# The steps of the 32x32 inversion on GpSimd instead of VectorE, in a hybrid decoder block

## Chip, cores and metric

The kernel runs on one core of a Trainium2 chip. The metric is the device time of one execution in microseconds (us). An execution under the hardware profiler gives the trace; its own time stands beside its span below. The engines are TensorE (PE; its weight loads are PEld), VectorE (DVE), ScalarE (ACT), GpSimd (POOL), and SyncE (SP), whose queue here only issues DMAs.

## What is computed

One layer of a decoder on 256 tokens and 16 meta tokens in front of them (L = 272), width 2048, all in float32. After a normalisation one large projection feeds three branches: RWKV-7 time mixing (16 heads of 64), a forgetting attention (FoX, 16 heads of 64) and gates. The two branches are projected, gated, added, projected again, and a SwiGLU network of width 5632 follows.

```
xn = rms(h, n1);  proj = xn @ w_in
y_a = rwkv7(...);  y_b = fox(...)
h = h + (g_a * (y_a @ w_a) + g_b * (y_b @ w_b)) @ w_o
h = h + (silu(gate) * up) @ w_dn          # gate, up = rms(h, n2) @ w_gu
```

The core of rwkv7 is a scan over tokens; for each head with a 64x64 state S:

```
sa = einsum('bhvk,bhk->bhv', S, a_t)
S  = S*w_t + sa*b_t + v_t*k_t
y_t = einsum('bhvk,bhk->bhv', S, r_t)
```

## The kernel before

**Projections.** Weights come from HBM in jobs. `wload` (L299) issues the DMA of a block of 128x1024 into `raw` on SP's queue (L318), makes a rounded copy `wh` on ScalarE (L322) and the remainder `wl` on VectorE (L323). `raw`, `wh` and `wl` have three buffers each. TensorE then multiplies with both parts (L333 to L335, L391 to L394). `run` (L377) loads the next job before it multiplies the last one.

**The recurrence.** The scan is done in chunks of 64 tokens, and each chunk needs the inverse of a unit triangular 64x64 matrix. The heads are taken in four groups `g` of four heads; a group has 16 such matrices (4 heads x 4 chunks) and 4 smaller ones for the meta tokens. For each group `rwkv_jobs(g)` (L615) runs the projections, and then `rwkv_bg(g)` (L670) runs as a stream in the background of the later projections: `slot` (L361) gives a stream a turn between TensorE's jobs, and each `yield` names the nanoseconds after which the stream is due again. So the order of TensorE's instructions is written by hand (`tc.manual_schedule`, L289). Outside the first stage, the order on the other engines, with SP's queue and GpSimd's, is laid out when the program is built.

**The inversion of the diagonal blocks.** In `rwkv_bg`:

- L765 to L773: the masked matrices `NK` go through DRAM (`d1`) into `ln`, so that each of 112 partitions holds one 32x32 block (1024 values). Three partition groups of 32 hold the same 32 blocks, one for each third of the result's rows; the last 16 hold the meta blocks.
- L830: GpSimd copies unit rows from `lunit` to `lx`, the result, with 11 rows of 32 in each partition.
- L831 to L838: 31 steps of forward substitution. Step `s_` multiplies column `s_` of the first n = s_//3+1 rows with row `s_` of the block into `lt` (L834), and adds that to the n rows in `lx` (L836). Both work on n lines of w = 31-s_ elements in 112 partitions. Every instruction needs the one before it.
- L841 to L848: the result goes through DRAM (`d2`, `d3`) into the 64x64 inverse `X` and `X0` for the meta tokens: seven DMAs out, six back, all on SP's queue.
- L913: VectorE transposes part of `X` into `XT`. L920 (`QT`) and L928 complete the off-diagonal blocks on TensorE; `step` (L854) then runs the recurrence. The line of most of these matmuls in the profile is that of the helper `pe_mm` (L355).

**Other work of GpSimd around the steps.** The copies of `NK` (L776, L780), the bonus term (L791), the biases and masks of the attention (L1067 to L1070, twice in a group), zeroing of tiles (L716, L738, L797, L828, L829), and the differences `zd` for the token shift (L445), which VectorE's L448 uses. At the start of the kernel it makes masks (L129, L138, L152, L154).

**Other work of VectorE there.** wl (L323), the sums of gate halves `zg` (L399, one operand in PSUM), scores and their division (L1087, L1098), and the scaling of the next group's projections (L437).

Of the kernel before, what the change touches and what calls it, by code (L numbers as in the profile page):

```python
# [13 lines left out]
ALU = mybir.AluOpType  # L14
# [42 lines left out]
LANES = 112  # L57
# [40 lines left out]
def hybrid_block(ctx, tc, A, out, dbg=None):  # L98
    nc = tc.nc
# [515 lines left out]
    def rwkv_jobs(g):  # L615
# [24 lines left out]
        def mul(w):  # L640
            (uh, ul), (gh, gl) = w
            gg = box["gg"] = ot(f"gg{g}")
            for m in range(2):
                ms = slice(m * P, (m + 1) * P)
                ps = main_ps(f"g{g}{m}")[:, :T]
                for k in range(2):
                    mm3(ps, gh[:, k, ms], gl[:, k, ms], sgh[:, k, :], sgl[:, k, :], k == 0, k == 1)
                nc.vector.tensor_copy(gg[:, m, :], ps)
            for nm, i, dh, dl, bname in (("sig", 0, twh, twl, "w0"), ("aa", 1, adh, adl, "a0")):
                dst = box[nm] = et(f"{nm}{g}")  # L650
                for m in range(2):
                    ms = slice(m * P, (m + 1) * P)
                    ps = (aux_ps if i == 0 else main_ps)(f"{nm}{g}{m}")[:, :L]
                    mm3(ps, uh[:, i, ms], ul[:, i, ms], dh, dl, True, True)
                    nc.scalar.activation(dst[:, m, :], ps, AF.Sigmoid, bias=vc(bname, 2 * g + m))
            spawn(rwkv_bg(g, box), HOP)
# [13 lines left out]
    def rwkv_bg(g, box):  # L670
# [91 lines left out]
        ln = rw.tile([LANES, 32, 32], F32, tag="ln", name=f"ln{g}", bufs=1)  # L762
# [62 lines left out]
        lx = rw.tile([LANES, 11, 32], F32, tag="lx", name=f"lx{g}", bufs=1)  # L825
# [5 lines left out]
        for s_ in range(31):  # L831
            n, w = s_ // 3 + 1, 31 - s_
            tv, xv = lt[:, 0:n, s_ + 1:], lx[:, 0:n, s_ + 1:]
            nc.vector.tensor_tensor(tv, lx[:, 0:n, s_:s_ + 1].to_broadcast([LANES, n, w]),  # L834
                                ln[:, s_:s_ + 1, s_ + 1:].to_broadcast([LANES, n, w]), op=ALU.mult)
            nc.vector.tensor_tensor(xv, xv, tv, op=ALU.add)  # L836
            if s_ % 4 == 3:
                yield STEP  # L838
        for j in range(3):
            n = 11 if j < 2 else 10  # L840
# [550 lines left out]
```

## Time and profile before

| | us |
|---|---|
| median of 3 runs | 1566.58 (1565.39 to 1569.84) |
| the profiled execution | 1564.75 |
| its span | 1563.0 |
| GpSimd (POOL) busy | 104.3 |
| VectorE busy | 1015.7 |
| ScalarE busy | 766.8 |
| instructions L834 and L836 | 124 each, 168 to 781 ns and 181 to 681 ns, between 123.8 and 536.8 us |

The page of the profile gives the busy time of each engine as a share of the span. The chain of waits is followed back from the last instruction, at each step to what released it. Groups of instructions have a line, an engine, the operation, out<-in by the program's names with the shapes, a count, then the busy time in us and the mean of one in ns, then the idle time ahead of them. The rows of a timeline have start in us, duration in us (of all, where "xN" follows), engine, line and operation. A row of the table by stage has the stretch, its length, the busy time of TensorE with its instructions, the granted clock, the share of the DMA engines and GB/s. "SPq" is SP's queue; its durations are those of issuing.

### The profile page before, as it was taken

The page shows a single profiled execution, that of the slowest core. Times are in us where ns is not written, and L with a number is a line of the kernel's source. Part 1 is how long each engine was busy: PE and PEld are TensorE (multiplying, and loading weights), DVE is VectorE, ACT ScalarE, POOL GpSimd, SP SyncE. Part 2 cuts the span into 40 slices and gives each one's busy share as a digit, 9 for nine tenths or more (in the row PEclk, how much of TensorE's full clock was granted, in tenths as well). Part 3 has the DMA queues.
Part 4 walks back from the last instruction along what each step waited for, and adds up shares of the span by engine and source line. Part 5 has one row for each costly group of instructions (what it writes and reads, how often), then busy time and mean ns, then how long its engine had stood idle before and what let it go on. Part 6 is the DMA issues. An engine that isn't in the chain of part 4 may idle for free.

```text
span 1563.0 us, 26173 instructions
## 1 busy us (share of the span) xinstructions
PE 1553.5 (99%) x10225; PEld 1366.3 (87%) x10225; DVE 1015.7 (65%) x1854; ACT 766.8 (49%) x1118; POOL 104.3 (7%) x194
## 2 busy tenths in 40 slices
PE   9999999999999999999999999999999999999998
PEld 9999988989889888999888888888888888888887
DVE  7878688677768856875655666566566656444443
ACT  6655455465445544654445554454445544333332
POOL 2121103102203100000000000000000000000000
PEclk9999999999999999999999999999999999999999
DMA  7556546546545566777666666666666666666664
GB/s 243 173 154 173 158 126 179 157 119 168 166 135 148 161 182 192 248 225 227 189 182 179 188 186 190 188 188 189 188 189 189 185 193 187 188 202 199 187 200 131
DMA packets 211483, 283.33 MB, mean 181 GB/s; under 512 B 23888, under 2 KB 128352, under 8 KB 211360
## 3 DMA queue, kind: packets, MB, share of 16 engines
q1 hardware_dynamic: 206752, 277.53, 60.8%
q10 hardware_dynamic: 4608, 4.13, 0.8%
q8 instruction: 80, 1.31, 0.4%
q14 instruction: 43, 0.35, 0.1%
HBM read 274.43 MB, written 7.19 MB: 180 GB/s over the span
## 4 chain that ended last, share of the span: by engine, by line
PE 94%; DVE 3%; DMA 1%; ACT 1%; issue 1%; SPq 0%; POOL 0%; DVEq 0%; ACTq 0%
PE up L392 10%; PE gt L392 10%; PE zg L392 7%; PE dn L1255 5%; PE dn L1253 5%; PE dn L1254 5%; PE up L394 5%; PE gt L394 5%; PE zg L394 3%; PE f L333 2%; PE f L392 2%; PE f L335 2%; PE f L334 2%; PE br L334 2%; PE br L335 2%; PE br L333 2%
## 5 line engine op out<-in xcount | busy, mean ns | idle before, releaser
L323 DVE TENSOR_TENSOR wl<-raw,wh 128x1024 fp32r<-128x1024 f32 (+1 forms) x496 | 605.3, 1221 | 439.7 <-ACT wh L322 437.8
L322 ACT ACTIVATE wh<-raw 128x1024 fp32r<-128x1024 f32 (+1 forms) x496 | 521.2, 1052 | 624.5 <-PE dn L1254 144.4
L392 PE MATMUL gt<-hts,wh 128*128 128x512 f32 x704 | 245.0, 394 | 0.0
L392 PE MATMUL up<-hts,wh 128*128 128x512 f32 x704 | 244.9, 394 | 0.0
L394 PE MATMUL gt<-hts,wl 128*128 128x256 f32 x660 | 186.2, 282 | 0.0
L394 PE MATMUL up<-hts,wl 128*128 128x256 f32 x660 | 186.0, 282 | 0.0
L392 PE MATMUL zg<-xhl,wh 128*128 128x512 f32 x512 | 184.3, 403 | 0.0
L392 PEld LDWEIGHTS up<-hts,wh 128*128 128x128 f32 x704 | 130.1, 188 | 26.4
L392 PEld LDWEIGHTS gt<-hts,wh 128*128 128x128 f32 x704 | 130.1, 188 | 26.3
L1254 PE MATMUL dn<-wh,acl 128*128 128x512 f32 x352 | 139.5, 396 | 0.0
L1253 PE MATMUL dn<-wh,ach 128*128 128x512 f32 x352 | 139.5, 396 | 0.0
L1255 PE MATMUL dn<-wl,ach 128*128 128x512 f32 x352 | 139.5, 396 | 0.0
L394 PE MATMUL zg<-xhl,wl 128*128 128x256 f32 x480 | 135.0, 281 | 0.0
L394 PEld LDWEIGHTS up<-hts,wl 128*128 128x128 f32 x660 | 124.7, 189 | 1.8
L394 PEld LDWEIGHTS gt<-hts,wl 128*128 128x128 f32 x660 | 124.7, 189 | 1.8
L392 PEld LDWEIGHTS zg<-xhl,wh 128*128 128x128 f32 x512 | 94.5, 188 | 20.8 <-issue 1.8
L394 PEld LDWEIGHTS zg<-xhl,wl 128*128 128x128 f32 x480 | 90.6, 189 | 1.1
L1255 PEld LDWEIGHTS dn<-wl,ach 128*128 128x128 f32 x352 | 66.3, 188 | 16.2
L1254 PEld LDWEIGHTS dn<-wh,acl 128*128 128x128 f32 x352 | 66.3, 188 | 16.2
L1253 PEld LDWEIGHTS dn<-wh,ach 128*128 128x128 f32 x352 | 66.3, 188 | 16.1
L333 PE MATMUL f<-xhl,wh 128*128 128x272 f32 x256 | 77.7, 303 | 0.0
L335 PE MATMUL f<-xhl,wl 128*128 128x272 f32 x256 | 73.8, 288 | 0.0
(459 smaller groups left out, 2777.6 us busy)
## 6 DMA issues: line engine op xcount, KB each, us to landing
raw<-in_w_gate_up_dram SPq DMA_DIRECT2D x176, 512.0 KB, 3.6
raw<-in_w_in_dram SPq DMA_DIRECT2D x160, 512.0 KB, 4.2
raw<-in_w_down_dram SPq DMA_DIRECT2D x88, 512.0 KB, 4.7
raw<-in_w_o_dram SPq DMA_DIRECT2D x32, 512.0 KB, 4.6
raw<-in_w_branch_a_dram SPq DMA_DIRECT2D x16, 512.0 KB, 3.9
raw<-in_w_branch_b_dram SPq DMA_DIRECT2D x16, 512.0 KB, 3.8
zgd<-zg ACTq DMA_DIRECT2D x30, 128.0 KB, 2.4
gate<-zgd SPq DMA_DIRECT2D x15, 256.0 KB, 5.8
```

The costliest lines, as they stand in the source:

```text
L322: nc.scalar.activation(wh[:prow, cs_], raw[:prow, cs_], AF.Copy)
L323: nc.vector.tensor_tensor(wl[:prow, cs_], raw[:prow, cs_], wh[:prow, cs_].bitcast(F32), op=ALU.subtract)
L333: nc.tensor.matmul(ps, wh, ah, start=first, stop=False)
L334: nc.tensor.matmul(ps, wh, al, start=False, stop=False)
L335: nc.tensor.matmul(ps, wl, ah, start=False, stop=last)
L392: nc.tensor.matmul(ps.rearrange("p (a t) -> p a t", a=2), wh, act, start=first, stop=last)
L394: nc.tensor.matmul(ps[:, :T], wl, act[:, 0, :], start=False, stop=False)
L1253: nc.tensor.matmul(box[t], ah[:, kt, ts_], wh[:, k, :], start=first, stop=False)
L1254: nc.tensor.matmul(box[t], al[:, kt, ts_], wh[:, k, :], start=False, stop=False)
L1255: nc.tensor.matmul(box[t], ah[:, kt, ts_], wl[:, k, :], start=False, stop=last)
```

## The change

The two instructions of each of the 31 steps are issued on GpSimd. Their operands, shapes and order stay as they are, and so does all else in the source: the copy to `lx` ahead of them, the yields, and the DMAs behind them.

```diff
         for s_ in range(31):
             n, w = s_ // 3 + 1, 31 - s_
             tv, xv = lt[:, 0:n, s_ + 1:], lx[:, 0:n, s_ + 1:]
-            nc.vector.tensor_tensor(tv, lx[:, 0:n, s_:s_ + 1].to_broadcast([LANES, n, w]),
-                                ln[:, s_:s_ + 1, s_ + 1:].to_broadcast([LANES, n, w]), op=ALU.mult)
-            nc.vector.tensor_tensor(xv, xv, tv, op=ALU.add)
+            nc.gpsimd.tensor_tensor(tv, lx[:, 0:n, s_:s_ + 1].to_broadcast([LANES, n, w]),
+                                    ln[:, s_:s_ + 1, s_ + 1:].to_broadcast([LANES, n, w]), op=ALU.mult)
+            nc.gpsimd.tensor_tensor(xv, xv, tv, op=ALU.add)
             if s_ % 4 == 3:
                 yield STEP
```

## The prediction

> **What bounds the kernel now.** I read the page first, for who is busy.
>
> ```profile
> span 1563.0 us, 26173 instructions
> ...
> PE 1553.5 (99%) x10225; PEld 1366.3 (87%) x10225; DVE 1015.7 (65%) x1854; ACT 766.8 (49%) x1118; POOL 104.3 (7%) x194
> ```
>
> TensorE (PE) is busy for 1553.5 of 1563.0 us. All its idle time together is 9.5 us, start included, so that is the most that any change away from TensorE can win. VectorE (DVE) at 65% is not the bound. Second, the chain of waits around the inversion. In the third of the four head groups it leaves TensorE:
>
> ```profile
> 406.38 0.19 DVE lx L836
> ...
> 406.59 0.61 SPq L841
> ...
> 411.74 1.69 DMA X<-d
> ...
> 415.48 4.61 DMA raw<-in_w_in_dram
> ...
> 420.19 1.06 ACT wh L322
> 421.25 0.41 ACT pT L1110
> 421.66 0.04 issue
> 421.71 1.41 PE po L355 x10
> ```
>
> This is read from top to bottom: the last step of the inversion releases the DMAs of the inverse on SP's queue; a weight load (raw, L318) stands behind them there; ScalarE waits for that load with wh, pT stands behind wh, and TensorE waits for pT. So the inversion's end already touches the path, through SP. Third, the table by stage shows what that costs:
>
> ```profile
> 416.00:455.00 39.00, 37.34 (x401) 1.00 0.57 166
> ```
>
> TensorE is idle for 1.66 of 39 us in that group, at full clock (1.00). This is the largest hole that an earlier end of the inversion could close.
>
> **What is removed.** Each group runs 31 steps of a multiplication and an addition. The groups of VectorE's instructions in the first group's inversion, from 123 to 153.4 us:
>
> ```profile
> L323 DVE TENSOR_TENSOR wl<-raw,wh 128x1024 fp32r<-128x1024 f32 x10 | 12.2, 1220 | 4.3 <-ACT wh L322 4.3
> L836 DVE TENSOR_TENSOR lx<-lx,lt 112x84 f32<-112x84 f32 (+23 forms) x31 | 7.6, 247 | 0.6
> L834 DVE TENSOR_TENSOR lt<-lx,ln 112x84 f32<-112x84 f32 (+23 forms) x31 | 7.6, 245 | 0.6
> L399 DVE TENSOR_TENSOR zg<-zg,zg 128x256 f32<-128x256 f32 x4 | 1.7, 417 | 1.3 <-ACT zg L398 1.3
> ```
>
> VectorE loses 15.2 us of work per group, 61 us in four. I put that at nothing: the 9.5 us above bound what it could give, and of the place shown it could give 1.66 us, if the weight load there came earlier.
>
> **What is added: the price of a step on GpSimd (POOL).** The shape of step s is n lines of w elements with n = s//3+1 and w = 31-s. Over the 31 steps that makes 1991 elements and 176 lines, twice (L834 and L836): 62 instructions, 3982 elements, 352 lines. The nearest rows of GpSimd are its other two-input operations and one that works on short lines:
>
> ```profile
> L445 POOL TENSOR_TENSOR zd<-z x24: 612/640/1611, 52.3 to 445.7; 128x272 f32<-128x272 f32 x16, 128x256 f32<-128x256 f32 x8
> ```
>
> ```profile
> 399.08 0.74 POOL L1070 TENSOR_TENSOR bias<-bias,cmask 128x256 f32<-128x256 f32 x1
> ```
>
> ```profile
> L138 POOL TENSOR_SCALAR_AFFINE_SELECT mup<-mup 64x64 f32<-64x64 f32 x4 | 0.8, 236 | 0.1
> ...
> L154 POOL TENSOR_SCALAR_AFFINE_SELECT lunit<-lunit 16x256 f32<-16x256 f32 x1 | 0.7, 732 | 0.1
> ...
> L129 POOL TENSOR_SCALAR_AFFINE_SELECT cmask<-cmask 128x128 f32<-128x128 f32 x1 | 0.3, 293 | 0.0
> ```
>
> In L445 (duration: least, median, most) I read 612 ns as the 256-element form and 640 as the 272-element form: 1.75 ns an element and 164 ns beside. Without a price for lines, 62 x 0.164 + 3982 x 0.00175 = 17.1 us: the lower end. L1070 does 256 elements in two lines, with a broadcast operand as in L834, in 0.74 us: 0.128 us more for one more line. 352 - 62 = 290 further lines at that price are 37 us: 54 us, the upper end. Between them lies the affine select: 293 - 236 ns for 64 more elements is 0.89 ns each, so 256 in one line would take 0.407 us; L154 does them in eight lines of 32 in 0.732, which is 0.047 us for each further line. I take that, because lines of about 32 elements are what the steps have: 290 x 0.047 = 13.6, in all 31 us for a group left alone, twice VectorE's own time. A step that waits for the one before it has its gap in this by counting whole durations, although unrelated instructions of GpSimd start a little before the last one ends.
>
> **It is not left alone.** The same instruction as above, in the first group, and what VectorE did then:
>
> ```profile
> 145.73 1.88 POOL L1070 TENSOR_TENSOR bias<-bias,cmask 128x256 f32<-128x256 f32 x1
> ```
>
> ```profile
> 145.79 1.21 DVE L323 TENSOR_TENSOR wl<-raw,wh 128x1024 fp32r<-128x1024 f32 x1
> ```
>
> 1.88 against 0.74 us: 1.14 longer, nearly the whole of the wl that ran beside it. So GpSimd stands while wl runs. Which of VectorE's other work stops it? Beside wl (L323) and zg (L399) of the rows above, the division of the scores (L1098) is there:
>
> ```profile
> L1098 DVE TENSOR_SCALAR s<-s,sums 128x144 f32<-128x144 f32 (+1 forms) x4 | 1.3, 322 | 0.0
> ```
>
> ```profile
> 397.31 1.11 POOL L1067 TENSOR_SCALAR bias<-bias,cq,hs 128x272 f32<-128x272 f32 x2
> ```
>
> ```profile
> 397.88 0.41 DVE L399 TENSOR_TENSOR zg<-zg,zg 128x256 f32<-128x256 f32 x1
> ```
>
> L399, which reads one operand from PSUM, kept its 0.41 us inside a busy stretch of GpSimd, so I count only wl and L1098: 12.2 + 1.3 = 13.5 of 30.4 us, 44%. GpSimd keeps 56%, and 31 us become 55. Were L399 to stop it too, it would be 15.2 of 30.4, a pace of 0.50.
>
> The Trainium skill (SBUF — State Buffer, Who interferes with whom) says the same against this change: VectorE and GpSimd share one pair of ports under a lock held for the whole instruction, taken by VectorE when it has two SBUF inputs or runs a two-port mode. By it L399 goes free and the pace is the 0.56 that I use; by a mere sharing of bandwidth the 31 us would stay 31 and nothing would come late. The trace agrees with the lock (1.88 against 0.74 us).
>
> **What lies on the path.** The first group's times, from the queues:
>
> ```profile
> 112.08 1.94 SPq L771 DMA_DIRECT2D ln<-d  x3
> ```
>
> ```profile
> DMA to landing us min/median/max: 3.8/4.4/5.0
> ```
>
> ```profile
> 139.60 12.23 SPq L318 DMA_DIRECT2D raw<-in_w_in_dram  x4
> 153.37 1.98 SPq L841 DMA_DIRECT2D d<-lx  x3
> ...
> 161.06 1.52 SPq L318 DMA_DIRECT2D raw<-in_w_in_dram  x3
> ```
>
> ```profile
> 153.16 0.18 DVE L836 TENSOR_TENSOR lx<-lx,lt 112x11 f32<-112x11 f32 x1
> ...
> 161.24 0.45 DVE L913 STREAM_TRANSPOSE XT<-X 128x256 f32<-128x256 f32 x1
> ```
>
> From the last addition (153.34) to the end of XT (161.69) are 8.35 us: seven DMAs out, the way back to X, the transposition. TensorE needs XT at QT, whose place in its order is written by hand; GpSimd is free for the steps once its bonus addition (L791) is over:
>
> ```profile
> 170.94 0.62 PE QT L355 x32
> ...
> 297.70 0.62 PE QT L355 x32
> ...
> 426.90 0.62 PE QT L355 x32
> ...
> 553.79 0.62 PE QT L355 x32
> ```
>
> ```profile
> 115.45 1.83 POOL L791 TENSOR_SCALAR bo<-bo,vcol 128x256 f32<-128x256 f32 x2
> ...
> 246.32 1.83 POOL L791 TENSOR_SCALAR bo<-bo,vcol 128x256 f32<-128x256 f32 x2
> ...
> 370.60 2.77 POOL L791 TENSOR_SCALAR bo<-bo,vcol 128x256 f32<-128x256 f32 x2 [1.64 <-DVE bo L790]
> ...
> 499.78 2.77 POOL L791 TENSOR_SCALAR bo<-bo,vcol 128x256 f32<-128x256 f32 x2 [1.64 <-DVE bo L790]
> ```
>
> Starts: 119 in the first group (ln lands up to 5.0 us after its last issue at about 114), then 248.2, 373.4, 502.6. When TensorE comes to QT, GpSimd has done 0.56 of the time since its start: 29.1, 27.7, 30.0 and 28.7 of 31 us. TensorE stops, VectorE runs out of wl, and the rest (1.9, 3.3, 1.0, 2.3) goes at full pace. With the 8.35 us behind, the stops are 10.2, 11.6, 9.4 and 10.7 us: 42 us. What waits behind GpSimd's steps on its own queue, the biases of the second head pair (L1067 to L1070) and the differences for the next group (L445), has TensorE's stop as its cover; without that cover a late L445 would hold VectorE at L448 and the wl behind it, and I price that within the same stop.
>
> The sum is made on the profiled execution, 1564.75 us with a span of 1563.0: 1564.75 + 42 = 1607. The median of the runs lies 1.83 us above it, so 1608 is the forecast.
>
> **Rivals.** *SP stands too early.* SP's order, and those of the other engines but TensorE, are laid out when the program is built, from estimates of durations. If these know 31 us and no lock, L841 stands at 119 + 31 = 150, behind the loads due then. In the trace SP issued no load for 9.2 us (151.83 to 161.06) without a stop in the first group. GpSimd has 22.5 us done when those are used up (159.2), ends at 167.7, and 7.7 later (as from 153.37 to 161.06) loads go on: 25.4 us, less 9.2, is a stop of 16 us, in four groups 65: 1630. With 17 us of work the same working gives 10 us a group: 1605. For it speaks the chain in the third group, where just this happens; against it, that the estimates may be longer than the truth.
>
> *It fits.* The one that is not slower: lines cost nothing and SP's order has room. Then 17.1/0.56 = 31 us end at 150, before VectorE's 153.3, and the 1.66 us hole may close: 1563 to 1567. The point from which it decides is X in time for QT: (170.94 - 8.35 - 119) x 0.56 = 24 us of work a group, 0.39 us an instruction. Against it speaks L1070, for it the slack of 9 us between XT (161.69) and QT.
>
> *Lines at the full price.* 54 us: 24.9 left at QT, stops of 33 us, about 1697. L1070 alone speaks for it; its mask operand may explain the difference as well.
>
> **How the numbers follow.** Forecast 0.40, SP too early 0.33, it fits 0.20, full price 0.07. A measurement of this kernel tells about 0.3% (4.7 us) from no change. The first two and the last are slower beyond that: 0.80, of which I move 0.02 to no change for stops that GpSimd's real price makes small. It fits is no change, but for 0.02 of a gain that adds up beyond the place that I priced: faster 0.02, within 0.20, slower 0.78. The range runs from 1565, for part of the case that fits, to 1660, which holds the forecast and SP's case with line prices up to 0.08 us (40 us a group left alone; the same working gives stops of 20 us, 1647); the full price is left out. For slower alone the forecast's own range is 1590 to 1640.
>
> **What would show it.** L834 and L836 on POOL with a mean near 0.5 us left alone, long ones beside every wl; 45 us or more from the first to the last; TensorE's stops four in number, before QT (by X) or at any matmul before it, with ScalarE waiting for raw (SP's case). VectorE falls by about 61 us. The forecast is wrong if a step costs under 0.39 us and X lands before QT, or if the stops are of more than 25 us.

## The result and the profile after

The changed kernel takes 1629.76 us (median of 4 runs, 1627.75 to 1631.44), the kernel before beside it 1565.99 (1564.43 to 1569.84): ratio 1.0403, 95% interval 1.038 to 1.0425. It is slower by 64 us. The profiled execution took 1627.75 us. The lines of its page that answer to those of before (the last is the granted clock in 40 slices):

```profile
span 1626.0 us, 26192 instructions
...
PE 1571.2 (97%) x10225; PEld 1378.8 (85%) x10225; DVE 969.8 (60%) x1606; ACT 766.3 (47%) x1118; POOL 200.5 (12%) x442
...
PEclk9998999899899979999999999999999999999999
```

The span grew by 63.0 us. TensorE's idle time went from 9.5 to 54.8 us (1626.0 - 1571.2), which is 45.3 of the 63. The other 17.7 are TensorE being busy for longer with the same 10225 matmuls, where the clock line dips.

Where TensorE stands, by its waits (total, times, longest):

```profile
PE po L355 <- ACT pT L1110: 22.9, 2, 11.8
PE k L333 <- ACT wh L322: 11.6, 2, 6.7
PE zg L392 <- ACT wh L322: 9.1, 2, 4.6
```

`po` is the product of the attention's probabilities `pT` with its values; `k` and `zg` are projections, which wait for a weight `wh`. All three rows lead to ScalarE: not one is QT waiting for X. The stops for pT are in the first two head groups (11.1 and 11.8 us), those for weights in the third and fourth. So the question is what ScalarE waited for:

```profile
ACT wh L322 <- DMA raw<-in_w_in_dram: 45.1, 16, 9.0
...
ACT pT L1110 <- DMA d<-lx: 26.7, 2, 13.7
```

The first row is a weight load that comes late. The second is ScalarE standing at pT until the inversion's own DMA lands: ahead of pT on its queue is the issue of the spill of gate values (L1155), which goes out at 154.45.

```profile
154.82 0.52 ACT L1110 ACTIVATE pT<-ppt 128x416 f32<-128x416 f32 x1 [13.00 <-DMA d<-lx]
```

SP's queue in the first group has both, the late loads and the DMA of the inversion:

```profile
114.95 19.76 SPq L318 DMA_DIRECT2D raw<-in_w_in_dram  x7
152.25 1.99 SPq L841 DMA_DIRECT2D d<-lx  x3
...
160.53 16.11 SPq L318 DMA_DIRECT2D raw<-in_w_in_dram  x7
```

In the kernel before, four more loads went out from 139.60 to 151.83 ahead of L841. Here L841 stands right behind the seventh load, SP waits at it from 134.7 until the inversion ends at 152.2, and no load is issued for 25.8 us. In this group the end of the inversion is no later than before (153.34); its place in the queue is earlier. What each stretch costs TensorE is in the table by stage (length, PE busy, ..., granted clock in the column before the DMA share):

```profile
121.00:153.00 32.00, 23.32 (x143) 19.77 (x141) 13.31 (x28) 12.06 (x23) 26.47 (x64) 0.92 0.31 91
153.00:172.00 19.00, 15.85 (x104) 15.10 (x106) 5.31 (x6) 5.39 (x8) 4.86 (x7) 0.78 0.58 154
...
441.00:460.00 19.00, 11.60 (x53) 10.41 (x53) 7.09 (x8) 4.57 (x6) 4.54 (x9) 0.63 0.61 177
...
582.00:604.00 22.00, 13.96 (x48) 10.51 (x49) 7.61 (x14) 6.92 (x10) 4.36 (x6) 0.61 0.67 190
```

X itself is in time. The rows of XT and QT give first and last start over the four groups:

```profile
L355 PE MATMUL QT<-XT,N x128: 191/191/212, 186.0 to 617.2; 32*32 32x32 f32 x128
L913 DVE STREAM_TRANSPOSE XT<-X x4: 445/445/446, 160.0 to 588.0; 128x256 f32<-128x256 f32 x4
```

XT starts at 160.0 and takes 0.445 us; QT begins at 186.0. XT is ready before 170.94, too, where QT stood in the kernel before.

And the steps (duration: least, median, most, then first and last start):

```profile
L834 POOL TENSOR_TENSOR lt<-lx,ln x124: 217/320/1421, 121.1 to 579.8; 112x84 f32<-112x84 f32 x12, 112x30 f32<-112x30 f32 x8, 112x54 f32<-112x54 f32 x8, 112x72 f32<-112x72 f32 x8
L836 POOL TENSOR_TENSOR lx<-lx,lt x124: 228/346/1461, 121.4 to 580.1; 112x84 f32<-112x84 f32 x12, 112x30 f32<-112x30 f32 x8, 112x54 f32<-112x54 f32 x8, 112x72 f32<-112x72 f32 x8
```

A median of about 0.33 us, with single ones of up to 1.46. Two of these long ones, and VectorE at the same time:

```profile
129.62 1.20 POOL L834 TENSOR_TENSOR lt<-lx,ln 112x88 f32<-112x88 f32 x1
130.90 1.43 POOL L836 TENSOR_TENSOR lx<-lx,lt 112x88 f32<-112x88 f32 x1
```

```profile
129.29 1.33 DVE L323 TENSOR_TENSOR wl<-raw,wh 128x1024 fp32r<-128x1024 f32 x1 [0.53 <-ACT wh L322]
...
130.88 1.21 DVE L323 TENSOR_TENSOR wl<-raw,wh 128x1024 fp32r<-128x1024 f32 x1
```

So three theories were put to the chip. *Queues*: the steps end late for the place that the build gave to whatever waits for them, and an in-order queue (SP's first) stands there with unrelated work behind it. *X late*, the forecast: GpSimd's price and the lock bring X too late for QT. *Lock*: the long steps are wl's doing. All ratios below are against runs of the kernel before on the same chip (medians of 1564.2 to 1564.7 us).

### The profile page after: what moved, and what is told of

Its sections match the earlier page's. It is cut to its first block, busy times and chain, and to the rows that moved or that the text cites. A ratio compares the mean times of both kernels' runs of the same rounds, so it can differ in the third digit from the quotient of the medians.

```text
span 1626.0 us, 26192 instructions
## 1 busy us (share of the span) xinstructions
PE 1571.2 (97%) x10225; PEld 1378.8 (85%) x10225; DVE 969.8 (60%) x1606; ACT 766.3 (47%) x1118; POOL 200.5 (12%) x442
## 4 chain that ended last, share of the span: by engine, by line
PE 84%; POOL 7%; DMA 3%; DVE 2%; issue 2%; ACT 1%; SPq 1%; ACTq 0%; POOLq 0%; DVEq 0%
PE up L392 10%; PE gt L392 10%; PE dn L1255 5%; PE dn L1254 5%; PE dn L1253 5%; PE up L394 5%; PE gt L394 5%; PE zg L392 4%; POOL lt L834 3%; POOL lx L836 3%; PE f L333 2%; PE f L392 2%; PE br L334 2%; PE br L333 2%; PE br L335 2%; PE wo L1254 2%
## 5 line engine op out<-in xcount | busy, mean ns | idle before, releaser
L392 PE MATMUL zg<-xhl,wh 128*128 128x512 f32 x512 | 188.8, 411 | 9.1 <-ACT wh L322 9.1
L394 PE MATMUL up<-hts,wl 128*128 128x256 f32 x660 | 186.0, 282 | 0.0
```

Of the source, the lines that this page charges most:

```text
L392: nc.tensor.matmul(ps.rearrange("p (a t) -> p a t", a=2), wh, act, start=first, stop=last)
L394: nc.tensor.matmul(ps[:, :T], wl, act[:, 0, :], start=False, stop=False)
```

## The experiments

**The place alone.** All steps are back on VectorE. The DMAs of the inverse stand on SP where the changed kernel has them, behind the seventh load, with the later loads behind them.

```diff
-                nc.sync.dma_start(v(raw)[sel], src)
+                with (tc.issue_after(lastinv[0]) if lastinv else ExitStack()):
+                    nc.sync.dma_start(v(raw)[sel], src)
...
+        yield 10000
         for j in range(3):
...
-            nc.sync.dma_start(X0[h * HD:h * HD + 16, :, 0:32], ...)
-        yield LANE
+            x_ = nc.sync.dma_start(X0[h * HD:h * HD + 16, :, 0:32], ...)
+            lastinv[:] = [getattr(x_, 'ins', x_)]
+        yield LANE - 10000
```

> The kernel before, all steps on VectorE, with the DMAs of the inverse (L841 to L848) set by hand where the changed kernel has them on SP: behind the seventh weight load of each group, the later loads behind them. GpSimd does nothing new. Theory of the queues (SP reaches L841 some 15 us before the inversion ends and stands, with the loads behind it): 1605 to 1640 us, with ScalarE waiting for raw. Rival (GpSimd's slower or blocked steps are themselves the cause): 1562 to 1575 us, as in the kernel before.

Measured: 1618.31 us, ratio 1.0339 (1.0321 to 1.0356), inside the expectation of the theory of the queues. Engines, SP's queue, the stage of the first stop and the largest wait of TensorE:

```profile
PE 1562.6 (97%) x10225; PEld 1373.2 (85%) x10225; DVE 1016.0 (63%) x1854; ACT 766.2 (47%) x1118; POOL 95.7 (6%) x194
```

```profile
115.87 19.82 SPq L319 DMA_DIRECT2D raw<-in_w_in_dram  x7
...
152.33 1.98 SPq L843 DMA_DIRECT2D d<-lx  x3
...
160.00 9.90 SPq L319 DMA_DIRECT2D raw<-in_w_in_dram  x6
```

```profile
153.00:172.00 19.00, 6.83 (x31) 6.29 (x30) 4.47 (x5) 3.34 (x4) 1.15 (x3) 0.65 0.57 155
```

```profile
PE k L334 <- ACT wh L323: 33.9, 3, 11.7
```

With a span of 1617.5 us TensorE is idle for 54.9 us; in the changed kernel it was 54.8. GpSimd does none of the steps here. The place on SP alone brings 54 us. All four stops here, 11.0 to 11.7 us, are for a weight; ScalarE has no wait for a DMA `d<-lx`. So the late loads are enough by themselves, and in the first two groups of the changed kernel ScalarE's own wait came ahead of them and covered them. The clock falls with the stop here too (0.65).

**The price and the lock by themselves.** A probe that runs nothing of the layer, executed once: the chain of 62 instructions on zeros, A on VectorE alone, B on GpSimd alone, then on GpSimd beside work of VectorE. C: ten subtractions of two 128x1024 SBUF tiles as wl, each followed by two additions that read PSUM. D: 40 of those additions. E: 20 subtractions back to back. F: ten one-operand scalings of 128x1024 and twenty additions.

```diff
+        g = phase("A", nc.vector, (), 0, gate)
+        g = phase("B", nc.gpsimd, (), 0, g)
+        g = phase("C", nc.gpsimd, (subs, halves, halves), 10, g)
+        g = phase("D", nc.gpsimd, (halves,), 40, g)
+        g = phase("E", nc.gpsimd, (subs,), 20, g)
+        g = phase("F", nc.gpsimd, (scale, halves, halves), 10, g)
```

> The steps by themselves on zeros, nothing of the layer is computed. Theory from the trace of the changed kernel: alone on GpSimd the 62 instructions take 21 to 25 us (0.22 to 0.40 us each and about 0.08 us between), on VectorE 14 to 17 us. My forecast had 31 us. Beside ten subtractions of two SBUF tiles (as wl) and twenty additions that read PSUM: 10 times 1.1 us longer, 32 to 36 us, if the subtraction locks GpSimd out. Beside 40 additions that read PSUM alone: no longer than alone, within 2 us. Beside 20 back to back subtractions: nothing of GpSimd proceeds while they run, about 24 us longer. Beside ten one-operand scalings and twenty additions: between, 22 to 36 us. Rival (bandwidth is merely shared): all of these within 10% of the time alone.

The multiplications of each phase (least, median, most; start of the first and of the last):

```profile
L36 DVE TENSOR_TENSOR ltA<-lxA,ln x31: 177/232/258, 9.1 to 24.8; 112x84 f32<-112x84 f32 x3, 112x30 f32<-112x30 f32 x2, 112x54 f32<-112x54 f32 x2, 112x72 f32<-112x72 f32 x2
```

```profile
L36 POOL TENSOR_TENSOR ltB<-lxB,ln x31: 215/310/355, 26.0 to 49.6; 112x84 f32<-112x84 f32 x3, 112x30 f32<-112x30 f32 x2, 112x54 f32<-112x54 f32 x2, 112x72 f32<-112x72 f32 x2
```

```profile
L36 POOL TENSOR_TENSOR ltC<-lxC,ln x31: 217/312/1387, 51.0 to 84.3; 112x84 f32<-112x84 f32 x3, 112x30 f32<-112x30 f32 x2, 112x54 f32<-112x54 f32 x2, 112x72 f32<-112x72 f32 x2
```

```profile
L36 POOL TENSOR_TENSOR ltD<-lxD,ln x31: 219/309/356, 85.6 to 109.3; 112x84 f32<-112x84 f32 x3, 112x30 f32<-112x30 f32 x2, 112x54 f32<-112x54 f32 x2, 112x72 f32<-112x72 f32 x2
```

```profile
L36 POOL TENSOR_TENSOR ltE<-lxE,ln x31: 217/318/22906, 110.6 to 156.9; 112x84 f32<-112x84 f32 x3, 112x30 f32<-112x30 f32 x2, 112x54 f32<-112x54 f32 x2, 112x72 f32<-112x72 f32 x2
```

```profile
L36 POOL TENSOR_TENSOR ltF<-lxF,ln x31: 218/335/816, 158.2 to 186.3; 112x84 f32<-112x84 f32 x3, 112x30 f32<-112x30 f32 x2, 112x54 f32<-112x54 f32 x2, 112x72 f32<-112x72 f32 x2
```

From the first to the last start: A 15.7, B 23.6, C 33.3, D 23.7, E 46.3, F 28.1 us; the last pair adds 0.5 on GpSimd. Alone, the steps cost 24 us, not the forecast's 31: a factor of 1.5 over VectorE. All six phases came out as expected; C and E exclude the rival, a mere sharing of bandwidth. One subtraction of two SBUF tiles costs GpSimd 0.97 us ((33.3 - 23.6)/10); an addition that reads PSUM costs it nothing (D against B); in E one multiplication of GpSimd lasts 22.9 us, through nearly all of the 20 subtractions. The Trainium skill (SBUF — State Buffer, Who interferes with whom) says that a VectorE instruction with at most one SBUF input, outside the two-port modes, leaves GpSimd alone, and that one with two SBUF inputs contends with GpSimd's reads; C, D and E agree. It also lets `tensor_scalar` contend in a two-port mode; F, 4.5 us longer than B, agrees that the scalings stop GpSimd at times.

**The lock inside the kernel.** wl of the loads around the inversion is left out; a scaled copy on ScalarE stands in its place, so the low halves of those weights are not the reference's.

```diff
-            nc.vector.tensor_tensor(wl[:prow, cs_], raw[:prow, cs_], wh[:prow, cs_].bitcast(F32), op=ALU.subtract)
+            if inv:
+                nc.scalar.activation(wl[:prow, cs_], raw[:prow, cs_], AF.Copy, scale=0.0001)
+            else:
+                nc.vector.tensor_tensor(wl[:prow, cs_], raw[:prow, cs_], wh[:prow, cs_].bitcast(F32), op=ALU.subtract)
...
+        inv.append(1)
...
+        yield 12000
+        inv.clear()
```

> The change as made, with the subtraction wl of the weight chunks that are loaded during the inversion left out and a scaled copy on ScalarE in its place, so that VectorE's wl does not run beside the steps (the low halves of those weights are not the reference's). Theory: without the lock the steps take 24 to 26 us from the first to the last in a group, against 31 us in the change as made, and the SP stop becomes shorter by some 7 us a group: 1590 to 1615 us, if ScalarE, which does about 1 us more for each chunk, does not become late itself. Rival (the long steps beside wl have another cause): the steps still take 30 us or more.

Measured: 1610.81 us, ratio 1.0295 (1.028 to 1.031). The first and the last step of the first group:

```profile
122.22 0.24 POOL L838 TENSOR_TENSOR lt<-lx,ln 112x31 f32<-112x31 f32 x1
```

```profile
146.32 0.23 POOL L840 TENSOR_TENSOR lx<-lx,lt 112x11 f32<-112x11 f32 x1
```

24.3 us, as in the probe, where the changed kernel has 31.1 (121.12 to 152.23). So the lock accounts for 7 us of a group, and the time is 19 us below the changed kernel's. Most of the loss stays, as SP still stands: here for 20.3 us without a load in the first group (134.08 to 154.38).

**Queued where the inversion really ends.** The changed kernel with the DMAs that carry the result behind the last load traced 20 us later in the program's order, three or four loads further; and the same for the kernel before.

```diff
-        for j in range(3):
+        yield 20000
+        with tc.issue_after(lastload[0].ins if hasattr(lastload[0], 'ins') else lastload[0]):
+            for j in range(3):
...
-        yield LANE
+        yield LANE - 20000
```

> The steps on GpSimd; the 13 DMAs stay on SP's queue, but are queued by hand behind the loads that SP had ahead of them in the kernel before (three or four loads later than in the change). Queue theory: 1566 to 1585, a few us left because the steps now end some us later than VectorE's did. Forecast's theory: X later still, 1607 to 1650. Lock theory: unchanged, about 1630.

> Control: the kernel before, steps on VectorE, with the same queueing by hand of the 13 DMAs. All theories: 1562 to 1570, since SP's order hardly moves.

Measured with the steps on GpSimd: 1586.35 us, ratio 1.0136 (1.0121 to 1.0151), two thirds of the loss gone and 1.4 us over the upper end of the expectation. With the steps on VectorE: 1563.49, ratio 0.999 (0.998 to 0.9999). On GpSimd SP is still early in the first group, with 18.1 us (145.63 to 163.69) without a load:

```profile
138.70 6.93 SPq L318 DMA_DIRECT2D raw<-in_w_in_dram  x3
156.01 1.99 SPq L842 DMA_DIRECT2D d<-lx  x3
...
163.69 1.52 SPq L318 DMA_DIRECT2D raw<-in_w_in_dram  x3
```

```profile
155.00:175.00 20.00, 12.98 (x84) 11.77 (x83) 8.36 (x25) 6.19 (x13) 5.97 (x16) 0.75 0.54 153
```

TensorE is idle for 7.0 of these 20 us, 6.4 of them in one stop for a weight. With its loads running, more of wl meets the steps: they now take 35 us.

**Off SP altogether.** The 13 DMAs on GpSimd's own queue, behind the steps; and the same for the kernel before. Then, in addition, XT behind the last wl traced, since the first of these runs showed it in the way.

```diff
-            nc.sync.dma_start(d2[:, j:j + 3 * n - 2:3, :], lx[32 * j:32 * j + 32, :n])
+            nc.gpsimd.dma_start(d2[:, j:j + 3 * n - 2:3, :], lx[32 * j:32 * j + 32, :n])
...
-        nc.vector.transpose(XT, X[:, :, 0:32])
+        with tc.issue_after(getattr(lastwl[0], 'ins', lastwl[0])):
+            nc.vector.transpose(XT, X[:, :, 0:32])
```

> The steps on GpSimd as in the change, and the 13 DMAs of the inverse (L841 to L848) issued on GpSimd's queue instead of SP's, so that no weight load stands behind them. Queue theory (the loss of 63 us comes from loads, and ScalarE's DMA of zg, standing behind DMAs placed for an earlier end): the stops go, 1566 to 1580. Forecast's theory (TensorE waits at QT for a late X): X is not earlier than before, GpSimd issues it itself, stops at QT stay, 1607 or more. Lock theory (GpSimd's reads hold up wl on VectorE, and that feeds TensorE): unchanged, about 1630.

> Control: the kernel before, steps on VectorE, with the same 13 DMAs issued on GpSimd's queue. Queue theory: the hole of 1.66 us in the third group closes, 1562 to 1567. Forecast's and lock theory say nothing of it: as before, 1566.

> The version with the DMAs of the inverse on GpSimd's own queue, and in addition the transposition XT set behind the last weight subtraction traced on VectorE, so that none of the three queues waits for the inversion early. Theory of the queues: 1566 to 1582 us, and no wait of TensorE for wl longer than 2 us is left that leads to XT. Rival (GpSimd is too slow, or its late end holds TensorE at QT): stays at 1600 us or more, with TensorE stopping at QT or the matmuls before it.

Measured: 1611.28 us without the move of XT, ratio 1.0296 (1.0279 to 1.0313), and 1612.05 with it, 1.0299 (1.0282 to 1.0317): both lie 30 us above what the theory of the queues expected, and by the number inside the ranges of its rival, X late. By the waits they are not: TensorE does not stop at QT in either. It stops ahead of it, in the first four times for wl (8.0 to 12.4 us), in the second for wl (5.6 to 7.9) and for the attention's scores (L1099, up to 11.9). Each of the longest stops follows a stand of VectorE's queue of 9.8 to 17.0 us. The control on VectorE's steps is 1568.96, 1.0029 (1.0019 to 1.0038), 2 us over its own expectation. VectorE's queue says why the first missed:

```profile
162.05 0.45 DVE L913 STREAM_TRANSPOSE XT<-X 128x256 f32<-128x256 f32 x1 [15.74 <-DMA X<-d]
```

VectorE stood for 15.74 us before XT, with wl behind it, which the matmuls needed. So a late X did stop TensorE here, by VectorE's queue and not by QT. And with XT moved:

```profile
170.31 0.50 DVE L448 SCALAR_TENSOR_TENSOR k<-zd,vcol,z 128x272 f32<-128x272 f32 x1 [13.09 <-POOL z L436]
```

Now it stood for 13.09 us before L448, whose `zd` (L445) was queued on GpSimd behind the steps, the DMAs and the biases. The stop moved from SP to VectorE twice. My theory had spoken of SP and ScalarE; these two runs add VectorE, at two places.

**ScalarE's part.** The spill of the gate values (L1155), whose wait for `d<-lx` held ScalarE, is issued by GpSimd.

```diff
-                    nc.scalar.dma_start(zgd[j, :, b, m, :], z)
+                    nc.gpsimd.dma_start(zgd[j, :, b, m, :], z)
```

> The change as made, with the spill of the gate values (L1155) issued by GpSimd and not by ScalarE, so that ScalarE no longer waits for a landing of the inverse. SP's order is the same. If SP's early L841 carries the loss and ScalarE's wait lies beside it, 1615 to 1632 us. If ScalarE's own wait carries it, 1570 to 1590 us.

Measured: 1640.75 us, ratio 1.0484 (1.0469 to 1.05): worse than the changed kernel, outside both expectations. TensorE's waits for pT are gone, and those for weights have grown by more:

```profile
PE k L333 <- ACT wh L322: 50.4, 3, 17.3
PE zg L392 <- ACT wh L322: 15.1, 1, 15.1
```

So SP's place does not need ScalarE's wait to cost the whole amount, as in the run of the place alone. The edit wasn't clean, though: two of the spills are now issued between the steps (at 138.10 and 144.03 in the first group), the steps take 33 us instead of 31, and SP stands for longer:

```profile
117.53 18.61 SPq L318 DMA_DIRECT2D raw<-in_w_in_dram  x7
155.98 2.00 SPq L841 DMA_DIRECT2D d<-lx  x3
...
164.14 1.54 SPq L318 DMA_DIRECT2D raw<-in_w_in_dram  x3
```

**Fewer steps on GpSimd.** The first 13 of 31.

```diff
-            nc.gpsimd.tensor_tensor(tv, ...)
+            eng = nc.gpsimd if s_ < 13 else nc.vector
+            eng.tensor_tensor(tv, ...)
```

> The first 13 of the 31 steps on GpSimd, the other 18 on VectorE. In this build the DMAs of the inverse stand on SP behind the same loads as in the kernel before, save one (7 and 3 loads in the first group, where the change as made has 7). Theory of the queues (the loss comes from where L841 stands on SP and what stands behind a late landing on the other engines): the inversion ends by about 155 us, the place fits, 1563 to 1573 us. Rival (the loss goes with the work that is handed to the slower engine): 26 of 62 instructions are handed over, so some 0.42 of 64 us, 1590 to 1595 us.

Measured: 1580.29 us, ratio 1.0098 (1.0083 to 1.0114), between the two expectations: neither holds. SP has its loads, but VectorE takes its turn at the hand-over too early and stands:

```profile
DVE lt L835 <- POOL lx L837: 16.6, 4, 5.0
```

**Nothing queued behind the steps.** First the subtraction `zd` of the hand-queued version moved to VectorE; then, in another run, also its memset (L436), the biases (L1067 to L1070), and the DMAs of the inverse one load later.

```diff
-            nc.gpsimd.memset(z[:rows, 0:1], 0.0)
+            nc.vector.memset(z[:rows, 0:1], 0.0)
...
-            nc.gpsimd.tensor_tensor(d[:rows, :n], pr, cu, op=ALU.subtract)
+            nc.vector.tensor_tensor(d[:rows, :n], pr, cu, op=ALU.subtract)
...
-        yield 20000
+        yield 22000
...
-            nc.gpsimd.tensor_tensor(bias[:, :, d1], bias[:, :, d1], cmb, op=ALU.add)
+            nc.vector.tensor_tensor(bias[:, :, d1], bias[:, :, d1], cmb, op=ALU.add)
```

> The version with the DMAs of the inverse queued by hand behind three more loads (1586 us), and in addition the differences zd (L445), which stand behind the steps on GpSimd, done on VectorE. Theory of the queues: the 19.5 us in which VectorE waited for zd go, and with them most of what was left of the loss: 1566 to 1578 us. Rival (what is left there is the price of GpSimd's late end, by X or by the loads): 1583 to 1590 us.

> The steps on GpSimd as in the change, but nothing that others wait for soon is queued behind them or ahead of their end: the DMAs of the inverse stand behind four or five more weight loads on SP, and the biases (L1067 to L1070) and the differences with their memset (L445, L436) are on VectorE. Theory of the queues: the late landing of X is covered by the slack ahead of QT, 1563 to 1572 us. Rival (the forecast's: X comes too late for QT, or the late end costs by itself): 1580 us or more, with TensorE stopping before QT.

The subtraction alone: 1584.87 us, 1.0127 (1.0112 to 1.0142), a miss, and inside the rival's range. VectorE's wait moved to the memset of the same tile, which GpSimd still had behind the steps:

```profile
DVE zd L445 <- POOL z L436: 15.3, 4, 4.7
```

TensorE's longest stop hardly changed: 6.1 us for a weight, 6.4 without the edit. So what was left there came by the loads, as the rival had it, and not by `zd`.

All of it: 1573.3 us, 1.0061 (1.0048 to 1.0075), 1.3 us over the expectation and well below the rival's 1580. The stage after the steps in each of the four groups:

```profile
155.00:175.00 20.00, 16.70 (x165) 14.74 (x164) 10.36 (x31) 8.42 (x19) 1.98 (x6) 1.00 0.55 157
...
290.00:315.00 25.00, 23.87 (x271) 21.97 (x270) 13.88 (x33) 11.35 (x23) 1.10 (x3) 1.00 0.59 168
...
420.00:440.00 20.00, 16.50 (x183) 14.75 (x182) 8.87 (x21) 7.18 (x13) 1.10 (x3) 0.91 0.60 177
...
550.00:575.00 25.00, 25.00 (x253) 20.62 (x251) 12.96 (x28) 12.99 (x26) 0.00 (x0) 1.00 0.64 183
```

In the first and third group 11 loads stand ahead of L842, in the second and fourth 12: idle 3.3 and 3.5 us against 1.1 and 0.0. No stop for a weight of 1 us or more is left. Which of the edits did it was not separated. One queue still stands: in the third group VectorE stands at XT for X for 4.70 us with the division of the scores (L1098) behind it, and TensorE's 3.43 us there are a wait for those scores; in the first group 1.30 us are. SP's rows of the first group in this version:

```profile
138.37 10.72 SPq L318 DMA_DIRECT2D raw<-in_w_in_dram  x4
156.45 1.99 SPq L842 DMA_DIRECT2D d<-lx  x3
...
164.14 1.53 SPq L318 DMA_DIRECT2D raw<-in_w_in_dram  x3
```

Set side by side, the time in which SP issues no load and TensorE's idle time in the stage of it, first group of each, with what TensorE waited for in its stops:

| kernel | no load (us) | TensorE idle (us) | waiting for (us) |
|---|---|---|---|
| before | 9.2 | 0 | |
| nothing queued behind | 15.0 (149.09 to 164.14) | 3.3 | pT 2.0, scores 1.3 |
| queued by hand | 18.1 | 7.0 | weights 7.0 |
| without wl beside the steps | 20.3 | 8.7 (2.1 + 6.5 in two stages) | weight 8.5 |
| place alone | 24.3 (135.69 to 160.00) | 12.2 | weights 12.2 |
| as changed | 25.8 | 11.8 (8.7 + 3.2 in two stages) | pT 11.1, weight 0.8 |
| spill on GpSimd | 28.0 (136.14 to 164.14) | 18.0 (153 to 175) | weights 18.0 |

In the four rows in which TensorE waits for weights, the weights in the buffers cover some 10 to 12 us of the pause; what goes beyond that, TensorE pays nearly one for one.

## Why the prediction was right and wrong

The measured time lies 22 us above the forecast and inside the range, and the sign was right, but the forecast's mechanism failed: the steps cost less than it had, and TensorE never stopped at QT for X. The rival *SP stands too early* happened, and its 1630 is the measured time.

- *VectorE's relief is worth nothing*: nothing speaks against it. The two rows of the steps (15.2 us a group) are gone from VectorE, and no version with them gone is faster than the kernel before. VectorE's busy time fell by 45.9 us and not 61. The durations of its instructions do add up to 60.5 us less (1080.3 to 1019.8); but busy time counts a stretch in which two of them overlap only once, and there was 64.6 us of such overlap before and 50.0 after.
- *"0.047 us for each further line"*: wrong, and the step that failed first. Alone the steps take 24 us, not 31. The affine select was the wrong neighbour: it had lines and another operation, and I gave the difference to the lines. In the probe, one line of 30 elements and ten lines of 3 cost the same 0.24 us:

```profile
26.65 0.24 POOL L36 TENSOR_TENSOR ltB<-lxB,ln 112x30 f32<-112x30 f32 x1
...
48.38 0.24 POOL L36 TENSOR_TENSOR ltB<-lxB,ln 112x30 f32<-112x30 f32 x1
```

  The lower end, 17.1 us, left out the gap between dependent instructions: 30 pairs in 23.6 us are 0.79 us a pair, of which the medians (0.31 and 0.33) are work, so some 0.07 us an instruction is gap.
- *The lock, and who takes it* (wl does, L399 with its PSUM operand does not): right, shown by the probe and by the run without wl.
- *Pace 0.56, 55 us*: wrong in size. Measured 31 us as changed and 35 with the loads running, which is a pace of 0.78 and 0.70. About half of the error is the price (24.3/0.56 would be 43), the rest the pace: as the loads stood, fewer wl ran beside the steps, and one costs them 0.97 us, less than its own 1.22.
- *"TensorE stops at QT"*: wrong. The term of 42 us in the forecast's sum did not occur: XT was there 25 us before QT in the first group. With 24 us of work alone the steps met the prediction's own deciding point, "X in time for QT".
- *SP too early*: right in kind. The order shows L841 behind the seventh load, where SP was done at 134.7. The working had put it at 150, by an estimate of 31 us (its second case, 17 us, would give 136), and the end of the steps at 167.7 where it was 152.2. Both are some 15 us off in the same direction, so that the pause came out right: 25.4 us against 25.8. The estimate itself is in no view; that it was short is read from the order. Of the 16 us a group that the working made of this pause, 11 were measured as idle time (45.3/4) and 4 as slower work of TensorE (17.7/4), which it did not have: the match of 1630 is largely luck. The sign that the prediction gave for this case, ScalarE waiting for raw, holds for the stops of the third and fourth group; those of the first two are ScalarE's wait for the inversion's DMA.
- Not foreseen: that the same early end was built into ScalarE's, VectorE's and GpSimd's own orders, so that taking SP out of the way uncovered the next. "a late L445 would hold VectorE at L448" stood in the prediction as something priced within the same stop; it was a stop of its own.

Left open: the changed kernel is 0.6% slower than the version with the place alone at the same idle time (54.8 and 54.9 us). The difference is in TensorE's busy time, 1571.2 against 1562.6. The changed kernel has six stops of more than 3 us, the other four. The version with the spill on GpSimd has four stops too, of 15.1 to 17.3 us, and a busy time of 1561.4. That points to the number of stops and the slower clock after each, and not to their length; no run varies the number alone.

No version with the steps on GpSimd came down to the kernel before. The best is 0.6% slower, and its inversion still ends 3 us later than VectorE's did (156.4 and 153.3 us in the first group). The fastest kernel of all is the one before with its DMAs queued by hand, 0.1% under it, at the edge of what its runs can tell.

## What to carry to other kernels

When an operation goes to another engine and the order of the queues is laid out at build time, look first for what is laid out to wait for its end, on every in-order queue, and count what stands behind each of them; this can weigh more than the operation's own duration. Compare the order of the queues of both builds before the durations: here seven loads ahead of L841 where there had been eleven was worth 54 of 64 us, with the inversion of the first group ending no later. To test it, move the place and leave the engine: give the old kernel the new place, and the new kernel the old one.

## What the runs showed of the hardware that was not expected

A stop of TensorE costs more than its length. In the four stages in which the stops ended the granted clock was 0.61 to 0.81, and the same matmuls kept TensorE busy 17.7 us longer. Short stops differ. With nothing queued behind, two of 1.30 and 1.97 us left the clock of their stage (155 to 175 us) at 1.00, and one of 3.43 us gave 0.91 (420 to 440 us). In the version queued by hand, though, stops of 2.01 and 1.12 us, 6 us apart, gave 0.91 as well. The Trainium skill (TensorE: Matmul & The Clock Gate, Why this matters for your kernels) advises against gaps of more than about 3 us, after which the clock falls back. The first two of these stages agree; the third shows a fall below that length.

In phase E of the probe GpSimd got nothing between two-operand instructions of VectorE that follow each other without a gap: one multiplication of some 0.24 us took 22.9 beside 20 of them. And a DMA issued from ScalarE's queue stood until a DMA of SP's queue had landed (26.7 us before pT in two places, as the profile infers the releaser), though the two share no data; with that DMA on another queue the wait was gone. Why it stood is not shown.
